# Mixer A/B of a hybrid trunk: turns of channel blocks by DMA in place of engine copies, and a new order of states, outputs, gate and projection

## The chip, the cores and the metric

The kernel runs on one core of a Trainium2 chip. The metric is the device time of one execution in microseconds (us); the median of three runs of the kernel before is 2035.25 us (2034.42 to 2035.31).

## What is computed

Two decoder layers over 512 tokens of width 1024. The change touches one place alone, the mixer of the first layer, where a short gated convolution (A) and a diagonal state space (B) share an input and an output projection:

```python
proj = h @ ab_w_in[j]
hc, gb, gc, u = jnp.split(proj, [CONV_CH, 2 * CONV_CH, 3 * CONV_CH], axis=-1)
ya = short_conv_mixer(hc, gb, gc, conv_w[j])        # gb * conv3(gc * hc)
yb = s5_mixer(u, ...)                               # 32 groups of 16 channels, 64 states each
mix = jnp.concatenate([ya, yb], axis=-1) @ ab_w_out[j]

# s5_mixer, after the scan over the tokens:
z = jax.nn.gelu(y)
out = z * jax.nn.sigmoid(z @ w_glu + b_glu)
```

The two feed-forward blocks, the layer norms, the second layer's attention and the gated embeddings are the same in both kernels.

## The kernel before, in words

Activations lie with channels on the partitions, in tiles of 128 channels by 512 tokens. Every product is made of three matmuls on high and low halves (`xh,whi`, `xl,whi`, `xh,wlo`), so a product of one 128-channel output tile over K = 1024 is 24 matmuls of 512 columns; the text calls it a whole. Weights come as a stream of 128 x 1024 pieces (`Stream`): SyncE issues a load into one of 3 raw buffers, ScalarE casts the high half (`whi`, L77), VectorE subtracts for the low half (`wlo`, L78), and the halves lie in a ring of 7. A load must wait for the `wlo` of the piece three earlier, since that frees its raw buffer. After each use of a piece, `free` issues one more load and one more split, so loads, casts and subtractions stand in their engines' queues at that place of the program.

The mixer's pieces are numbered here w0 to w25: w0 to w3 make the four tiles of u (`group`), then for ct = 0 to 3 come `hc`, `gc` and `gb` (hc0 is w4, gc0 w5, gb0 w6, ... gb3 w15), then the gate (`w_glu`), the first half of the output projection and its tail. `hc` is copied out of PSUM by ScalarE (L832); `gc` is multiplied and convolved by VectorE (L839 to L843); `gb` is multiplied in (L848), and the result split into `Y`. The four PSUM banks "U" hold the results of wholes in turn.

The state space needs time on another axis: groups of 32 channels by every fourth token. A turn moves sixteen blocks of 32 partitions x 128 between a tile and its turned form, `ut` from `us` and `z` from `y`. Before, each turn is 16 copies (L764), 8 on ScalarE and 8 on VectorE. For a tile f of u:

- `states(f)`: 8 products from `ut[f]` and `pack[f]` into two banks "D" (L777; the trace counts 16 records), then on VectorE 6 multiplications and additions, 8 scans, and 6 more, into `hz[f]` (L783 to L805).
- `output(f)`: 12 products (24 records) into a bank "L" (L815, L817), Gelu on ScalarE (`y`, L819), the turn to `z[f]`, the split into `Y`, and the load of `pack[f+2]` (1792 KB, L744), which takes the place of `pack[f]`; there are two pack buffers.

The gate is 48 matmuls over all of `z` and a sigmoid, a product and a split for each tile (L868, L869). The first half of the output projection has eight outputs (`down`), added to `u` (L422). The `tail` then makes the second half together with the layer norm; it opens with L143. `self.at(ns, f)` puts f into the order when `ns` of matmul time have been written behind it.

The order of the work is written by hand, in `plan`. A turn of the tiles of u is called `along`.

Of the kernel before, what the change touches and what calls it, by code (L numbers as in the profile page):

```python
# [10 lines left out]
F = mybir.dt.float32  # L11
R = mybir.dt.float32r
I32 = mybir.dt.int32
AF = mybir.ActivationFunctionType
OP = mybir.AluOpType

P = 128
T = 512
# [181 lines left out]
class Program:  # L200
# [23 lines left out]
    def pair(self):  # L224

        return tuple(self.pairs.tile([P, KD, T], R, name=f"x{s}", tag=f"x{s}") for s in "hl")
# [502 lines left out]
    def mixer_ab(self, ln):  # L729
        nc, ws, a = self.nc, self.ws, self.a  # L730
        v = nc.vector
        es = ExitStack()
        pool = es.enter_context(self.tc.tile_pool(name="ab", bufs=1))
        small = pool.tile([P, 16], F, name="small")
        nc.gpsimd.dma_start(small, a["abs"])
        bglu, cw = small[:, 0:4], small[:, 4:16].rearrange("p (c j) -> p c j", j=3)
        ut = [pool.tile([P, 4, P], F, name=f"ut{f}") for f in range(4)]
        us, z = {}, {}
        Y = self.pair()
        packs = {}  # L740

        def load(f):
            packs[f] = pool.tile([P, 3584], F, name="pack", tag="pack", bufs=2)
            nc.sync.dma_start(packs[f], self.s5d[f])  # L744

        load(0)
        load(1)

        def have_u(m, b):
            for i in range(2):  # L750
                us[m + i] = pool.tile([P, 4, P], F, name="us", tag="uz", bufs=4)
                nc.scalar.copy(us[m + i], b[i].rearrange("p (k t) -> p t k", t=4))
            if m == 0:
                along(0)

        def along(f):

            x = us.pop(f)
            turn_steps(lambda q, t: (ut[f][32 * t:32 * t + 32, q, :], x[32 * q:32 * q + 32, t, :]))

        def turn_steps(pair):
            for q in range(4):
                for t in range(4):
                    (nc.scalar.copy if t % 2 else nc.vector.tensor_copy)(*pair(q, t))  # L764

        self.group(have_u)
        self.pending = False
        hz = {}

        def states(f):  # L770
            pk = packs[f]
            SB = pk[:, 1024:2048].rearrange("p (r q s) -> p r q s", r=2, q=4)
            b = [self.bank("D") for _ in range(2)]
            uu = ut[f]
            for r in range(2):
                for q in range(4):
                    nc.tensor.matmul(b[r][:, q * P:(q + 1) * P], lhsT=SB[:, r, q, :], rhs=uu[:, q, :],  # L777
                                     start=True, stop=True)
            c, s = pk[:, 0:512], pk[:, 512:1024]
            t1 = self.work.tile([P, 2, T], F, name="m1", tag="t4")  # L780
            t2 = self.work.tile([P, 2, T], F, name="m2", tag="t4")
            zz = pool.tile([P, 2, T], F, name="zz")
            v.tensor_mul(t1[:, 0], b[0], c)  # L783
            v.tensor_mul(t1[:, 1], b[1], s)
            v.tensor_add(zz[:, 0], t1[:, 0], t1[:, 1])
            v.tensor_mul(t2[:, 0], b[1], c)
            v.tensor_mul(t2[:, 1], b[0], s)
            v.tensor_sub(zz[:, 1], t2[:, 0], t2[:, 1])
            for r in range(2):
                for q in range(4):  # L790
                    x = zz[:, r, q * P:(q + 1) * P]
                    v.tensor_tensor_scan(x, self.s5r[:, 4 * f + q:4 * f + q + 1].to_broadcast([P, P]), x, 0.0,  # L792
                                         op0=OP.mult, op1=OP.add)
            h = pool.tile([P, 2, 4, P + 2], F, name="hz", tag="hz", bufs=2)
            hz[f] = h
            nc.gpsimd.memset(h[:, :, :, 0:1], 0.0)
            t1 = self.work.tile([P, 2, T], F, name="m1", tag="t4")
            t2 = self.work.tile([P, 2, T], F, name="m2", tag="t4")
            v.tensor_mul(t1[:, 0], zz[:, 0], c)
            v.tensor_mul(t1[:, 1], zz[:, 1], s)  # L800
            v.tensor_mul(t2[:, 0], zz[:, 0], s)
            v.tensor_mul(t2[:, 1], zz[:, 1], c)
            t1, t2 = (t.rearrange("p r (q k) -> p r q k", q=4) for t in (t1, t2))
            v.tensor_sub(h[:, 0, :, 1:P + 1], t1[:, 0], t1[:, 1])
            v.tensor_add(h[:, 1, :, 1:P + 1], t2[:, 0], t2[:, 1])  # L805

        def output(f):
            pk = packs.pop(f)
            CB = pk[:, 2048:3072].rearrange("p (r q s) -> p r q s", r=2, q=4)
            KB = pk[:, 3072:3584].rearrange("p (q s) -> p q s", q=4)  # L810
            b = self.bank("L")
            h = hz.pop(f)
            for q in range(4):
                o = b[:, q * P:(q + 1) * P]
                nc.tensor.matmul(o, lhsT=KB[:, q], rhs=ut[f][:, q], start=True, stop=False)  # L815
                for r in range(2):
                    nc.tensor.matmul(o, lhsT=CB[:, r, q], rhs=h[:, r, q, 0:P], start=False, stop=r == 1)  # L817
            y = self.work.tile([P, 4, P], F, name="y", tag="t4")
            nc.scalar.activation(y.rearrange("p q k -> p (q k)"), b, AF.Gelu_apprx_tanh)  # L819
            z[f] = pool.tile([P, T], F, name="z", tag="uz", bufs=4)  # L820
            zf = z[f].rearrange("p (k t) -> p t k", t=4)
            turn_steps(lambda q, t: (zf[32 * q:32 * q + 32, t, :], y[32 * t:32 * t + 32, q, :]))
            self.split_pair(Y, 4 + f, z[f])
            if f + 2 < 4:
                load(f + 2)

        conv = {}

        def hc(ct):
            b = self.whole()  # L830
            conv[ct] = pool.tile([P, T], F, name="hc")
            nc.scalar.copy(conv[ct], b)  # L832

        def gc(ct):
            b = self.whole()
            uu = pool.tile([P, T + 2], F, name="uu")
            vv = pool.tile([P, T], F, name="vv")
            nc.gpsimd.memset(uu[:, 0:2], 0.0)
            v.tensor_mul(uu[:, 2:], conv[ct], b)  # L839
            conv[ct] = vv  # L840
            v.tensor_scalar(vv, uu[:, 0:T], cw[:, ct, 0:1], None, op0=OP.mult)
            for j in (1, 2):
                v.scalar_tensor_tensor(vv, uu[:, j:j + T], cw[:, ct, j:j + 1], vv, op0=OP.mult, op1=OP.add)  # L843

        def gb(ct):
            b = self.whole()
            vv = conv.pop(ct)
            v.tensor_mul(vv, vv, b)  # L848
            self.split_pair(Y, ct, vv)

        plan = [(hc, 0), (along, 1), (states, 0), (along, 2), (gc, 0), (along, 3), (states, 1), (gb, 0), (hc, 1),
                (output, 0), (gc, 1), (output, 1), (gb, 1), (states, 2), (hc, 2), (gc, 2), (states, 3), (gb, 2),
                (hc, 3), (output, 2), (gc, 3), (output, 3), (gb, 3)]
        for f, i in plan:
            f(i)

        self.lows()
        banks = []
        for i in range(2):
            w = ws.take()  # L860
            for s in range(2):
                b = self.bank("U")
                self.mm(b, w, Y, range(4 * s, 4 * s + 4), range(4, 8), slice(0, T))
                banks.append(b)
            ws.free()
        for f in range(4):
            t = self.work.tile([P, 2, T], F, name="gl", tag="t4")
            nc.scalar.activation(t[:, 0], banks[f], AF.Sigmoid, bias=bglu[:, f:f + 1])  # L868
            v.tensor_mul(t[:, 1], t[:, 0], z[f])  # L869
            self.split_pair(Y, 4 + f, t[:, 1])  # L870
        self.lows()
        for j in range(KD):
            if j % 2 == 0:
                w = ws.take()
            self.down(w, (j % 2) * 4, Y, range(4), j, True)
            if j % 2:
                ws.free()
        self.tail(Y, 4, ln)
        es.close()

# [365 lines left out]
def cut_rows(w, k0, k1):  # L1246

    k, m = w.shape
    n = 8 // (k1 - k0)
    w = w.reshape(k // P, P, m // P, P)[k0:k1].transpose(1, 2, 0, 3)  # L1250
    return [w[:, j:j + n].reshape(P, 1024) for j in range(0, m // P, n)]
# [21 lines left out]
def pieces_ab(w_in, w_glu, w_out):  # L1273
    t = tiles_of(w_in)
    out = t[12:16]
    for c in range(4):
        out += [t[c], t[8 + c], t[4 + c]]
    return out + cut_rows(w_glu, 0, 4) + cut_rows(w_out, 0, 4) + cut_tail(w_out, 4)


def pieces_ple(wp, wg):
# [117 lines left out]
```

## Time and profile before

| | |
|---|---|
| median of the three runs | 2035.25 us |
| the profiled execution, its own time | 2035.52 us |
| its span, first to last instruction | 2033.8 us |
| TensorE busy (matmuls) | 98% of the span |
| VectorE, ScalarE, GpSimd busy | 52%, 34%, 5% |
| granted TensorE clock, mean | 0.993 |

Times in the rows count from the start of the span. The mixer's work that the change touches runs from 408.6 us (the first tiles of u are done) to 553.2 us (the tail opens). The granted clock is 1.00 in nearly all of the span; it has two levels, 1.2 and 2.4 GHz, and a mean between 0.5 and 1 in a stretch is a mix of the two.

### The profile page before, as it was taken

The numbers are of one execution on the slowest core, as the hardware profiler recorded it, in microseconds if no ns is written. First come the engines' busy times: TensorE is split into PE (matmuls) and PEld (weight loads), VectorE is DVE, ScalarE is ACT, GpSimd is POOL, SyncE is SP. The second block draws the span as 40 slices with busy tenths as digits, with TensorE's granted clock in tenths as the row PEclk, the third lists the DMA queues.
The fourth block names the chain that finished last, engine by engine and source line by source line (L and its number), as shares of the span: only waits on it lengthen the run. The fifth ranks groups of instructions, "written<-read, shape, count | busy, mean of one in ns | idle before, by whom it ended". The sixth has DMA issues, their size and how long they took to land.

```text
span 2033.8 us, 23989 instructions
## 1 busy us (share of the span) xinstructions
PE 1986.0 (98%) x9550; PEld 1645.0 (81%) x9550; DVE 1066.5 (52%) x2027; ACT 684.1 (34%) x1026; POOL 94.3 (5%) x89
## 2 busy tenths in 40 slices
PE   9999999999899999999999999998999999999999
PEld 7888888877688888887888888887777888888877
DVE  6457554678554333336645554356986543333363
ACT  5222332444343222224432222234444432222242
POOL 0001110000000000000000000002431000000000
PEclk9999999999899999999999999999999999999999
DMA  6234343323314232321332322312211142323312
GB/s 218 95 104 145 115 134 114 126 89 129 99 37 137 91 103 89 104 99 42 119 114 85 105 101 87 104 69 83 74 52 45 49 135 93 104 84 103 103 42 73
DMA packets 54736, 197.99 MB, mean 97 GB/s; under 512 B 6529, under 2 KB 6817, under 8 KB 54113
## 3 DMA queue, kind: packets, MB, share of 16 engines
q1 hardware_dynamic: 51840, 187.74, 27.5%
q0 software_dynamic: 2640, 8.67, 1.2%
q8 instruction: 75, 1.23, 0.3%
q14 instruction: 37, 0.30, 0.0%
q10 hardware_dynamic: 144, 0.05, 0.0%
HBM read 187.00 MB, written 9.44 MB: 97 GB/s over the span
## 4 chain that ended last, share of the span: by engine, by line
PE 64%; DVE 8%; ACT 4%; issue 2%; POOL 0%; DMA 0%; DVEq 0%; ACTq 0%; POOLq 0%
PE U L260 44%; PE D L260 15%; PE D L443 1%; PE U L443 1%; DVE wlo L78 1%; ACT u L188 1%; ACT whi L77 1%; PE D L1110 1%; ACT lnt L173 1%; PE U L1079 1%; DVE xl L197 0%; DVE lnst L150 0%; PE L L180 0%; ACT xh L190 0%; DVE zz L792 0%
## 5 line engine op out<-in xcount | busy, mean ns | idle before, releaser
L260 PE MATMUL U<-xh,whi 128*128 128x512 f32 (+1 forms) x2000 | 751.4, 376 | 6.3 <-ACT xh L319 5.3
L260 PE MATMUL U<-xl,whi 128*128 128x512 f32 (+1 forms) x2000 | 745.2, 373 | 5.4 <-DVE xl L326 4.1
L260 PE MATMUL U<-xh,wlo 128*128 128x512 f32 (+1 forms) x2000 | 744.3, 372 | 0.0
L78 DVE TENSOR_TENSOR wlo<-wraw,whi 128x1024 fp32r<-128x1024 f32 (+1 forms) x321 | 393.6, 1232 | 303.3 <-ACT whi L77 301.8
L77 ACT CAST whi<-wraw 128x1024 fp32r<-128x1024 f32 (+1 forms) x337 | 350.6, 1045 | 559.7 <-PE D L260 309.3
L260 PEld LDWEIGHTS U<-xh,whi 128*128 128x128 f32 x2000 | 378.0, 189 | 76.5 <-ACT xh L319 6.4
L260 PEld LDWEIGHTS U<-xl,whi 128*128 128x128 f32 x2000 | 377.9, 189 | 73.9 <-DVE xl L326 6.4
L260 PEld LDWEIGHTS U<-xh,wlo 128*128 128x128 f32 x2000 | 377.8, 189 | 65.1
L260 PE MATMUL D<-xh,whi 128*128 128x512 f32 x608 | 237.6, 391 | 1.4 <-DVE u L422 1.0
L260 PE MATMUL D<-xh,wlo 128*128 128x512 f32 x608 | 236.6, 389 | 0.0
L260 PE MATMUL D<-xl,whi 128*128 128x512 f32 x608 | 236.6, 389 | 0.0
L373 DVE SCALAR_TENSOR_TENSOR gt<-gt,U 128x512 f32<-128x512 f32 x88 | 60.4, 687 | 265.8 <-PE U L260 208.8
L319 ACT CAST xh<-gt 128x512 fp32r<-128x512 f32 x88 | 54.6, 620 | 387.9 <-DVE gt L373 387.9
L260 PEld LDWEIGHTS D<-xh,whi 128*128 128x128 f32 x608 | 114.1, 188 | 27.7 <-DVE u L424 3.0
L260 PEld LDWEIGHTS D<-xh,wlo 128*128 128x128 f32 x608 | 114.2, 188 | 23.9
L260 PEld LDWEIGHTS D<-xl,whi 128*128 128x128 f32 x608 | 114.2, 188 | 23.3
L424 DVE TENSOR_TENSOR u<-u,D 128x512 f32<-128x512 f32 x64 | 43.9, 687 | 112.2 <-PE D L260 112.2
L422 DVE SCALAR_TENSOR_TENSOR u<-u,D 128x512 f32<-128x512 f32 x40 | 27.4, 687 | 108.1 <-PE D L260 108.1
L326 DVE TENSOR_TENSOR xl<-gt,xh 128x512 fp32r<-128x512 f32 x88 | 60.3, 685 | 8.2 <-ACT xh L319 8.2
L372 ACT ACTIVATE gt<-U 128x512 f32<-128x512 f32 x88 | 51.9, 589 | 18.4 <-PE U L260 18.3
L186 DVE TENSOR_SCALAR u<-L,lnw 128x128 f32<-128x128 f32 x96 | 32.8, 404 | 32.6 <-PE L L180 32.6
L173 ACT ACTIVATE lnt<-D,lnm,lny 128x512 f32<-128x512 f32 x24 | 17.4, 773 | 72.3 <-DVE lnm L170 72.3
(318 smaller groups left out, 1593.3 us busy)
## 6 DMA issues: line engine op xcount, KB each, us to landing
wraw<-wts SPq DMA_DIRECT2D x333, 512.0 KB, 3.5
pack<-s5d SPq DMA_DIRECT2D x4, 1792.0 KB, 9.4
s5d<-big POOLq DMA_DIRECT2D x20, 256.0 KB, 5.0
u<-x SPq DMA_DIRECT2D x8, 256.0 KB, 5.3
s5d<-big POOLq DMA_DIRECT2D x4, 512.0 KB, 3.3
out<-u SPq DMA_DIRECT2D x7, 256.0 KB, 2.0
wraw<-wts SPq DMA_DIRECT2D x4, 256.0 KB, 5.5
pt<-p POOLq DMA_DIRECT2D x2, 512.0 KB, 4.5
```

What stands on the lines that cost most here:

```text
L77: self.nc.scalar.copy(hi, t)
L78: self.lo_engine.tensor_sub(lo, t, hi.bitcast(F))
L173: p.nc.scalar.activation(self.z[:, c], self.banks[c], AF.Identity, bias=m, scale=y)
L186: p.nc.vector.tensor_scalar(out, x, gam, bet, op0=OP.mult, op1=OP.add)
L260: self.nc.tensor.matmul(out, lhsT=p[:, s], rhs=q[:, xk, cols], start=first and i == 0 and j == 0, stop=last and i == n - 1 and j == 2)
L319: self.nc.scalar.copy(hi[:, j, :], src)
L326: self.nc.vector.tensor_sub(out, src, hi)
L372: nc.scalar.activation(t[:, 0], pa, AF.Silu)
L373: nc.vector.scalar_tensor_tensor(t[:, 1], t[:, 0], 0.5, pb, op0=OP.mult, op1=OP.mult)
L422: self.nc.vector.scalar_tensor_tensor(u, u, ALPHA, d, op0=OP.mult, op1=OP.add)
L424: self.nc.vector.tensor_add(u, u, d)
L443: self.nc.tensor.matmul(b, lhsT=x, rhs=y, start=False, stop=k == TAIL - 1 and j == 2)
```

## The change

Three things. The turns are 16 DMAs of 32 x 128 each, from SBUF to SBUF, in place of 16 copies: on SyncE's queue, for `ut[0]` alternately on SyncE's and ScalarE's. A tile of `z` now has its tokens in turned order, and the gate's product puts them back (a view with a stride of four). The order is a new one: `states(0)` is put into hc0 (1500 ns after it begins), `states(1)`, (2), (3) behind gb0, gb1, gb2, `output(0)`, (1), (2) behind gc1, gc2, gc3, and `output(3)` behind the second output of the projection. Turns of `z` are put 1500 ns behind their output, the splits of `z` 9000 ns. Six of the projection's eight outputs are made before the gate's products, two behind them; the pieces of `w_out` and `w_glu` change places to suit.

```diff
+        def turn(out, src, engines):
+            for j in range(4):
+                for i in range(4):
+                    engines[(4 * j + i) % len(engines)].dma_start(out[32 * i:32 * i + 32, j, :], src[32 * j:32 * j + 32, i, :])
...
             for i in range(2):
-                us[m + i] = pool.tile([P, 4, P], F, name="us", tag="uz", bufs=4)
-                nc.scalar.copy(us[m + i], b[i].rearrange("p (k t) -> p t k", t=4))
-            if m == 0:
-                along(0)
-        def along(f):
-            x = us.pop(f)
-            turn_steps(lambda q, t: (ut[f][32 * t:32 * t + 32, q, :], x[32 * q:32 * q + 32, t, :]))
-        def turn_steps(pair):
-            for q in range(4):
-                for t in range(4):
-                    (nc.scalar.copy if t % 2 else nc.vector.tensor_copy)(*pair(q, t))
+                us = pool.tile([P, 4, P], F, name="us", tag="uz", bufs=4)
+                nc.scalar.copy(us, b[i].rearrange("p (k t) -> p t k", t=4))
+                turn(ut[m + i], us, (nc.sync,) if m + i else (nc.sync, nc.scalar))
...
-            z[f] = pool.tile([P, T], F, name="z", tag="uz", bufs=4)
-            zf = z[f].rearrange("p (k t) -> p t k", t=4)
-            turn_steps(lambda q, t: (zf[32 * q:32 * q + 32, t, :], y[32 * t:32 * t + 32, q, :]))
-            self.split_pair(Y, 4 + f, z[f])
+            z[f] = pool.tile([P, 4, P], F, name="z", tag="uz", bufs=4)
+            self.at(1500, turn, z[f], y, (nc.sync,))
+            self.at(9000, lambda: self.split_pair(Y, 4 + f, z[f].rearrange("p t k -> p (t k)")))
...
-        plan = [(hc, 0), (along, 1), (states, 0), (along, 2), (gc, 0), (along, 3), (states, 1), (gb, 0), (hc, 1),
-                (output, 0), (gc, 1), (output, 1), (gb, 1), (states, 2), (hc, 2), (gc, 2), (states, 3), (gb, 2),
-                (hc, 3), (output, 2), (gc, 3), (output, 3), (gb, 3)]
-        for f, i in plan:
-            f(i)
+        self.at(1500, states, 0)
+        for ct in range(4):
+            for i, f in enumerate((hc, gc, gb)):
+                f(ct)
+                n = 3 * ct + i
+                if n in (2, 5, 8):
+                    states(n // 3 + 1)
+                if n in (4, 7, 10):
+                    output(n // 3 - 1)
...
             self.down(w, (j % 2) * 4, Y, range(4), j, True)
             if j % 2:
                 ws.free()
+            if j == 1:
+                output(3)
+            if j == 5:
+                self.flush()
+                gates()
```

On SyncE's queue, from the first two packs on (`wraw` a weight piece, `pack<-s5d_1396` and `_1397` the third and fourth pack), the kernel before has:

```order
L744 DMA pack<-s5d_1395 128x3584
L70 DMA wraw<-wts 128x1024 x10
L744 DMA pack<-s5d_1396 128x3584
L70 DMA wraw<-wts 128x1024
L744 DMA pack<-s5d_1397 128x3584
L70 DMA wraw<-wts 128x1024 x252
```

The changed kernel has, in the same place:

```order
L744 DMA pack<-s5d_1395 128x3584
L70 DMA wraw<-wts 128x1024 x2
L753 DMA ut_3055<-us 32x128 x8
L753 DMA ut_3056<-us 32x128 x16
L70 DMA wraw<-wts 128x1024 x2
L753 DMA ut_3057<-us 32x128 x16
L753 DMA ut_3058<-us 32x128 x16
L70 DMA wraw<-wts 128x1024 x7
L744 DMA pack<-s5d_1396 128x3584
L753 DMA z<-y 32x128 x16
L70 DMA wraw<-wts 128x1024 x3
L744 DMA pack<-s5d_1397 128x3584
```

The ten pieces ahead of the third pack are w6 to w15 before and the eleven of the change w6 to w16. Of the pieces, w8 and w9 now stand behind the turns of the first two tiles, w10 to w16 behind all four; the fourth pack moved from behind w16 to behind w19. Each DMA of the change also waits, on its queue, for the landing of the one issued eight before it, by the semaphores that the build gives them.

On VectorE, from the second chain of states on (`hz` is what `output(1)` waits for), the kernel before has:

```order
L804 TENSOR_TENSOR hz<-m_3529 128x4x128
L805 TENSOR_TENSOR hz<-m_3530 128x4x128
L78 TENSOR_TENSOR wlo<-wraw,whi 128x1024
L848 TENSOR_TENSOR vv<-vv,U 128x512
L78 TENSOR_TENSOR wlo<-wraw,whi 128x1024
L326 TENSOR_TENSOR xl<-vv,xh 128x512
L764 COPY z<-y 32x128 x8
```

The changed kernel has between the first chain's end and the second chain's start, and behind its end:

```order
L801 TENSOR_TENSOR hz<-m_3432 128x4x128
L78 TENSOR_TENSOR wlo<-wraw,whi 128x1024 x2
L834 TENSOR_TENSOR uu<-hc,U 128x512
L836 TENSOR_SCALAR vv<-uu,small 128x512
L838 SCALAR_TENSOR_TENSOR vv<-uu,small,vv 128x512 x2
L78 TENSOR_TENSOR wlo<-wraw,whi 128x1024
L843 TENSOR_TENSOR vv<-vv,U 128x512
L779 TENSOR_TENSOR m_3543<-D,pack 128x512
...
L801 TENSOR_TENSOR hz<-m_3563 128x4x128
L78 TENSOR_TENSOR wlo<-wraw,whi 128x1024
```

The first `wlo` behind the second chain is that of w12 before and that of w13 in the change; the three `wlo` between the two chains are those of w10, w11 and w12, together with the convolution of gc0 and the product of gb0. Ahead of the first chain stand the `wlo` of w8 and w9 in the change, of w8 to w10 before.

## Rows read from the trace of the kernel before

**Rows 1.** The page's busy times by engine, over the whole span.

```profile
PE 1986.0 (98%) x9550; PEld 1645.0 (81%) x9550; DVE 1066.5 (52%) x2027; ACT 684.1 (34%) x1026; POOL 94.3 (5%) x89
```

**Rows 2.** Waits of PE, 340 to 640: who waited for whom, total us, times, longest.

```profile
PE U L260 <- ACT xh L319: 4.9, 1, 4.9
PE U L260 <- DVE xl L326: 3.7, 2, 2.0
...
PE D L777 <- DVE m L786: 2.6, 1, 2.6
PE D L777 <- issue: 2.0, 1, 2.0
PE L L817 <- DVE hz L804: 1.4, 1, 1.4
PE D L777 <- DMA pack<-s5d: 1.3, 1, 1.3
```

**Rows 3.** Timeline of PE, 408 to 560: start, us, line, records [idle before].

```profile
411.68 0.40 PE L260 MATMUL U<-xh,whi 128*128 128x512 f32 x1
...
417.14 1.95 PE L777 MATMUL D<-ut,pack 128*128 128x128 f32 x16
418.84 0.48 PE L260 MATMUL U<-xh,whi 128*128 128x512 f32 x1
...
441.55 0.38 PE L815 MATMUL L<-ut,pack 128*128 128x128 f32 x2
...
444.14 0.48 PE L260 MATMUL U<-xh,whi 128*128 128x512 f32 x1
...
476.26 3.65 PE L777 MATMUL D<-ut,pack 128*128 128x128 f32 x16 [2.04 <-issue]
479.66 0.48 PE L260 MATMUL U<-xh,whi 128*128 128x512 f32 x1
...
553.15 0.60 PE L143 MATMUL D<-ident,u 128*128 128x128 f32 x4
```

**Rows 4.** Busy us by engine in a stretch, then granted clock, DMA share, GB/s.

```profile
475.00:480.00 5.00, 3.74 (x18) 3.73 (x19) 4.96 (x13) 2.60 (x4) 0.00 (x0) 0.66 0.04 16
```

**Rows 5.** Line L764, the turn's copies: ns min/median/max, first and last start.

```profile
L764 DVE COPY ut<-us x32: 207/218/222, 409.3 to 441.6; 32x128 f32<-32x128 f32 x32
L764 ACT COPY ut<-us x32: 293/296/299, 409.7 to 430.0; 32x128 f32<-32x128 f32 x32
L764 ACT COPY z<-y x32: 409/414/429, 457.7 to 512.1; 32x128 f32<-32x128 f32 x32
L764 DVE COPY z<-y x32: 264/272/278, 457.7 to 515.1; 32x128 f32<-32x128 f32 x32
```

**Rows 6.** Timeline of SyncE's DMA queue, 445 to 480.

```profile
453.11 0.33 SPq L70 DMA_DIRECT2D wraw<-wts  x1
453.49 0.42 SPq L744 DMA_DIRECT2D pack<-s5d  x1
```

**Rows 7.** From issue to landing, lines L70 (weights), L744 (packs), L1230 (output).

```profile
DMA to landing us min/median/max: 3.3/3.5/8.0
...
DMA to landing us min/median/max: 7.7/9.4/12.3
...
DMA to landing us min/median/max: 1.7/2.0/2.1
```

**Rows 8.** Timeline of DVE, 405 to 460, around the first two chains of states.

```profile
424.25 0.69 DVE L783 TENSOR_TENSOR m<-D,pack 128x512 f32<-128x512 f32 x1
...
434.25 1.83 DVE L764 COPY ut<-us 32x128 f32<-32x128 f32 x8
...
437.25 0.68 DVE L839 TENSOR_TENSOR uu<-hc,U 128x512 f32<-128x512 f32 x1
...
440.01 1.83 DVE L764 COPY ut<-us 32x128 f32<-32x128 f32 x8
...
451.87 1.22 DVE L78 TENSOR_TENSOR wlo<-wraw,whi 128x1024 fp32r<-128x1024 f32 x1
```

More of the change, by code (lines that the diff above doesn't have):

```diff
@@ L737, in mixer_ab @@
         ut = [pool.tile([P, 4, P], F, name=f"ut{f}") for f in range(4)]
-        us, z = {}, {}
+        z = {}
         Y = self.pair()
@@ L849, in gb, with gates @@
             self.split_pair(Y, ct, vv)
-        plan = [(hc, 0), (along, 1), (states, 0), (along, 2), (gc, 0), (along, 3), (states, 1), (gb, 0), (hc, 1),
-                (output, 0), (gc, 1), (output, 1), (gb, 1), (states, 2), (hc, 2), (gc, 2), (states, 3), (gb, 2),
-                (hc, 3), (output, 2), (gc, 3), (output, 3), (gb, 3)]
-        for f, i in plan:
-            f(i)
[L857 to L870, printed above, removed]
+        def gates():
+            self.lows()
+            banks = []
+            for i in range(2):
+                w = ws.take()
+                for s in range(2):
+                    b = self.bank("U")
+                    self.mm(b, w, Y, range(4 * s, 4 * s + 4), range(4, 8), slice(0, T))
+                    banks.append(b)
+                ws.free()
+            for f in range(4):
+                t = self.work.tile([P, 2, T], F, name="gl", tag="t4")
+                nc.scalar.activation(t[:, 0], banks[f], AF.Sigmoid, bias=bglu[:, f:f + 1])
+                v.tensor_mul(t[:, 1].rearrange("p (k t) -> p t k", t=4), t[:, 0].rearrange("p (t k) -> p t k", t=4), z[f])
+                self.split_pair(Y, 4 + f, t[:, 1])
+        self.at(1500, states, 0)
[7 more added lines that the diff above has]
+                    output(n // 3 - 1)
         self.lows()
@@ L877, in mixer_ab @@
                 ws.free()
+            if j == 1:
[3 more added lines that the diff above has]
+                gates()
+        self.lows()
         self.tail(Y, 4, ln)
@@ L1277, in pieces_ab @@
         out += [t[c], t[8 + c], t[4 + c]]
-    return out + cut_rows(w_glu, 0, 4) + cut_rows(w_out, 0, 4) + cut_tail(w_out, 4)
+    first = cut_rows(w_out, 0, 4)
+    return out + first[:3] + cut_rows(w_glu, 0, 4) + first[3:] + cut_tail(w_out, 4)
 def pieces_ple(wp, wg):
```

## The prediction

> **What bounds the kernel now.** I read the page's busy times first: TensorE is busy for 98% of the span, so only a stretch where it idles can give anything [rows 1]. The waits of TensorE around the mixer name that stretch: six kinds, 4.9 + 3.7 + 2.6 + 2.0 + 1.4 + 1.3 = 15.9 us [rows 2]. The first two end on the split of z or vv into Y (L319, L326), behind copies of a turn; the third and fourth are states that wait for a turn or for VectorE.
>
> The timeline then prices the stage. A whole takes 417.14 - 411.68 = 5.46 us, 0.2275 a matmul; the products of one states 418.84 - 417.14 = 1.70; of one output 444.14 - 441.55 = 2.59 [rows 3]. From hc0 to the tail there are 12 wholes, 4 states, 4 outputs, 48 gate matmuls and eight outputs of 12 matmuls: 65.5 + 6.8 + 10.4 + 10.9 + 21.8 = 115.4 us. It takes 553.15 - 411.68 = 141.5 [rows 3]. So 26.1 us are lost: 15.9 in those waits, the rest mostly in slow matmuls behind them. One such place: after 2.04 idle the states took 479.66 - 476.26 = 3.40 in place of 1.70, in a stretch whose mean granted clock is 0.66 of 2.4 GHz [rows 3, 4]. With every wait gone the kernel would gain 26; the question is which waits the new order makes.
>
> **The copies removed.** ScalarE loses 32 x 0.296 + 32 x 0.414 = 22.7 us, VectorE 32 x 0.218 + 32 x 0.272 = 15.7 [rows 5]. Neither is on the path by itself; what they free is the head of Y's splits, and those waits (8.6 us) go. Moving output(3) behind two projections and the gate behind six does the same for z3. I charge nothing there: z3 has four projections, 10.9 us, between its Gelu and the gate.
>
> **The turns added.** A turn is 16 DMAs of 16 KB. The trace has no such DMA. Bounds for a turn: by landing, eight may be in flight and the output's stores land in 2.0 us at the median [rows 7], so two rounds, 4.0 us. By issue, two neighbours on SyncE start 453.49 - 453.11 = 0.38 apart [rows 6], so 16 x 0.38 = 6.1. Those move 128 rows where a turn's move 32, so the issue should be cheaper than that row; I take 5.0.
>
> The landing row is the one that a page speaks to. The Trainium skill ("DMA: Bandwidth & Descriptors", section on the anatomy of one DMA) gives a DMA a fixed part of about 2.0 us and says in its measured table that transfers under 64 KB are dominated by descriptors, which speaks against 128 of them; by its formula an estimate is 2.04 us for 16 KB and 4.1 for a turn, and the gain below would be 8.3 in place of 7.4. The shortest landing here, 1.7, agrees in size, though for stores to memory and not SBUF to SBUF [rows 7].
>
> What a turn delays is the queue behind it. us0 is there at 409.3, the first start of a copy of it [rows 5]. ut0 lands two rounds later, about 413.8 to 414.4; states(0) is placed 9 matmuls into hc0, at 413.7, so 0.5 us wait. ScalarE issues eight of these DMAs in order, so us1 is copied only at about 412.8. ut1 then takes SyncE to 417.8, and only there come w8 and w9 (before, w8 was loaded long ahead). They land 3.5 later [rows 7], the second about 1.3 behind the first; cast and subtraction take 1.1 and 1.2. w9's wlo ends at about 424.9.
>
> **VectorE's chain sets the packs.** In the new order the first chain of states stands behind that wlo: it starts at 424.9, against 424.25 before [rows 8], though its products are done by 416. The chain takes 434.25 - 424.25 = 10.0 [rows 8]. Behind it: wlo of w10 and w11 (1.15 each), convolution 440.01 - 437.25 = 2.76 [rows 8], wlo of w12 and the product of gb0 1.75, the second chain 10.0, wlo of w13 1.15. That is 424.9 + 10.0 + 2.3 + 2.76 + 1.75 + 10.0 + 1.15 = 452.9. Only then may w16 be issued, and the third pack stands behind w16 on SyncE: issue at 453.3. The kernel before shows the same queueing: its third pack went out at 453.49, right behind a weight that waited for the wlo of 451.87 to 453.09, though output(0) had left the buffer at 444.14 [rows 3, 6, 8]. The shortest pack landing is 7.7 [rows 7], and I take that, since no other pack is in flight: 461.0.
>
> What changed is who waits. Before, output(1) stood between; states(2) waited 1.3 [rows 2]. Now states(2) comes one whole after output(0). TensorE: 414.2 + 1.7 (states(0)) + 3.4 (rest of hc0) + 10.9 + 1.7 (states(1)) + 10.9 + 2.6 (output(0)) + 5.5 = 450.9. It waits 461.0 - 450.9 = 10.1 us.
>
> **The rest of the stage.** After that wait the clock is low: states(2) 3.4 as at 476.26 and 0.5 more in hc2, so 464.4 and 475.8 after hc2 and gc2, 478.4 after output(1). z0's DMAs follow the third pack and land about 463 to 465, ahead of the m tile that takes y's buffer (VectorE, about 472). w16's wlo ends about 476.3, ahead of 478.4, so w19 and the fourth pack go out at 478.5 and land at 486.2; gb2 ends at 483.9: a wait of 2.3, and 2.2 again for the clock. From 486.2: 3.4 + 0.5 + 10.9 + 2.6 + 5.5 (gb3) + 5.4 + 2.6 (output(3)) + 10.9 + 10.9 (gate) + 5.4 = 544.3. Each change of tile costs about 0.1 more at its first matmul, some 12 of them: 545.5. The chain sigmoid, product, split for the gate runs beside the last two projections (5.4 us) and its last split is wanted 2 us into the tail; I charge 0.3. The tail opens at 545.8 in place of 553.15: **a gain of 7.4 us**. The rest of the program is bound by TensorE and keeps its time.
>
> The profiled execution's own time is 2035.52 (span 2033.8 and 1.7 around it); less 7.4 it is 2028.1. Against the median, 0.3 lower, I forecast **2027.8**.
>
> **Rivals.** First, **slow turns**, which end slower than before. Up to a turn of 5.5 us only ut1 counts, 1 us for 1 us. Beyond it w10 is late, behind ut2 and ut3: it is issued at 413.6 + 3 turns, its wlo ends 5.7 later, VectorE stands still between the chains, and hc0's copy, which is queued on ScalarE behind w10's cast, holds a U bank. The third pack lands 25.0 behind that wlo. At 6.1 a turn this is 462.6 and the gain 5.8; at 8.1, 0.5 us a DMA, it is nothing; at 10 it is 474.3, 13.3 later, which is 5.9 slower than before: 2041. For it: weights on a shared queue land in up to 8.0 us [rows 7], and eight in flight at 5 us each is 10 a turn. Against it: 0.38 an issue and 2.0 a landing.
>
> Second, **late packs**: if both land in the 12.3 of the longest pack landing [rows 7] and not in 7.7, TensorE waits 4.6 longer twice: 2027.8 + 9.2 = 2037.0. For it: turns share the queue and the memory ports with the packs. Against: that longest one had another pack ahead of it.
>
> Third, **the whole gain**: the packs are there in time. Then about 6 us of the 26.1 remain, for ut0 and the tile changes: 2015. It would need the third pack out by 443, and VectorE's queue above denies it by 10 us.
>
> **How the numbers follow.** Forecast (2021 to 2032; a turn of 4.0 to 6.5 us, packs of 7.7 to 9.4): 0.58. Slow turns (2036 to 2046): 0.16. Late packs (2032 to 2038): 0.16. The whole gain (2013 to 2021): 0.10. About 0.2%, 4.1 us, is what a measurement of this kernel can tell from no change. Faster by more, below 2031.2: 0.10 and nearly all of 0.58, with little of late packs, 0.66. Slower by more, above 2039.3: most of slow turns and little else, 0.16. Within: 0.18. The range 2018 to 2038 leaves out about half of the third rival and most of the first.
>
> **What would show it.** In the changed kernel's trace: a wait of about 10 us of TensorE at the third states, ended by the pack, and one of about 2 at the fourth; the third pack issued right behind a weight load and a wlo, near 453; the first chain of states starting near 425, behind w9's wlo; no long wait on Y's splits at the gate; a turn of 4 to 6 us on SyncE; the tail opening near 546. Wrong would be: a pack landing before 451, a first chain starting with its products at 416, or a turn above 8 us.

## The result: 0.77% slower

| | before | after |
|---|---|---|
| median, us | 2035.28 (2034.42 to 2035.93, 4 runs) | 2050.86 (2049.72 to 2052.08, 4 runs) |
| ratio after / before, 95% interval | | 1.0077 [1.0059, 1.0094] |
| span of the profiled execution, us | 2033.8 | 2047.9 |
| the tail of the projection opens, us | 553.15 [rows 3] | 567.11 |

The forecast was 2027.8 with a range to 2038.0, so the sign is wrong. The span grew by 14.1 us and the opening of the tail moved by 13.96: the loss lies inside the stage that the prediction looked at, and the rest of the program kept its time.

The computing engines have no more work than before; ScalarE lost 22 us of copies (684.1 busy before, [rows 1]). The page of the changed kernel, busy times:

```profile
PE 1986.2 (97%) x9550; PEld 1644.6 (80%) x9550; DVE 1052.7 (51%) x1963; ACT 661.6 (32%) x962; POOL 94.4 (5%) x89
```

What grew are waits. The waits of TensorE in the changed kernel, 340 to 660 (who waited for whom: total us, times, longest), to be held against [rows 2]:

```profile
PE D L773 <- DMA z<-y: 10.6, 1, 10.6
PE U L260 <- ACT hc L827: 8.5, 1, 8.5
PE D L773 <- issue: 3.9, 1, 3.9
...
PE D L773 <- DMA pack<-s5d: 2.3, 1, 2.3
PE U L260 <- DVE xl L326: 2.3, 1, 2.3
PE D L143 <- DVE u L422: 1.5, 1, 1.5
PE D L773 <- DMA ut<-us: 1.2, 2, 0.6
PE U L260 <- ACT xh L319: 0.4, 1, 0.4
```

The 4.9 on `xh` and 3.7 on `xl` of before are nearly gone, as the change would have it. In their place stand 10.6 at the third states, 8.5 at a U bank and 3.9 at the second states: 30.7 in these eight rows, 15.9 in the six of [rows 2].

The first row is a lesson in reading: L773 computes states from `ut` and `pack` and never touches z. The wait is put down to the last transfer that landed; it is the pack that the states needed. The pack landed 7.8 us after its issue at 472.00, at 479.8, and the states started at 480.03. SyncE's own queue shows what held that pack up (start, us from the first to the end of the last issue, DMAs):

```profile
409.89 16.04 SPq L753 DMA_DIRECT2D ut<-us  x24
426.03 1.00 SPq L70 DMA_DIRECT2D wraw<-wts  x2
427.12 21.31 SPq L753 DMA_DIRECT2D ut<-us  x32
448.53 23.38 SPq L70 DMA_DIRECT2D wraw<-wts  x7
472.00 0.38 SPq L744 DMA_DIRECT2D pack<-s5d  x1
...
521.96 10.02 SPq L753 DMA_DIRECT2D z<-y  x16
```

A row is to be divided by its count: 21.31 / 32 = 0.67 us from one DMA to the next, 10.02 / 16 = 0.63. A turn costs SyncE 10.0 to 10.7 us, in place of 5.0. (The first two turns of z took 13.8 and 13.6: their eighth DMA waits for the landing of the pack issued eight before it, and SyncE's waits for the pack are 3.1 and 2.3 us.) All 56 of the u turns go ahead of w10 to w16, and the third pack stands behind w16: it is issued at 472.00, where the forecast had 453.3. The line of the turns itself, ns of one issue (min, median, max), then us from issue to landing:

```profile
L753 SPq DMA_DIRECT2D ut<-us x56: 507/588/1528, 409.9 to 447.8; - x56
...
DMA to landing us min/median/max: 1.7/1.8/7.6
```

They land in 1.8 us at the median, so none of the u turns had to wait for the landing of the one eight before it (eight issues take 5 us). What takes the time is issuing them one after the other. Nor did the turns slow the weights on their way: from 405 to 580 us a weight landed 3.4, 3.8 and 5.1 us after its issue (least, median, most), against 3.4, 3.6 and 5.8 before.

The way from w10 to TensorE, in the timelines of ScalarE, VectorE and TensorE of the changed kernel (start, us, line, operation, records [idle before and what ended it]):

```profile
452.22 1.04 ACT L77 CAST whi<-wraw 128x1024 fp32r<-128x1024 f32 x1 [19.89 <-DMA wraw<-wts]
453.17 0.58 ACT L827 COPY hc<-U 128x512 f32<-128x512 f32 x1
```

```profile
453.29 1.22 DVE L78 TENSOR_TENSOR wlo<-wraw,whi 128x1024 fp32r<-128x1024 f32 x1 [9.73 <-ACT whi L77]
...
470.34 1.21 DVE L78 TENSOR_TENSOR wlo<-wraw,whi 128x1024 fp32r<-128x1024 f32 x1
```

```profile
453.80 0.79 PE L260 MATMUL U<-xh,whi 128*128 128x512 f32 x1 [8.46 <-ACT hc L827]
...
480.03 3.75 PE L773 MATMUL D<-ut,pack 128*128 128x128 f32 x16 [10.64 <-DMA z<-y]
...
505.69 2.02 PE L773 MATMUL D<-ut,pack 128*128 128x128 f32 x16 [2.34 <-DMA pack<-s5d]
...
567.11 0.66 PE L143 MATMUL D<-ident,u 128*128 128x128 f32 x4 [1.53 <-DVE u L422]
```

w10's cast ends ScalarE's idle 19.9 us; the copy of hc0 is queued right behind it, and TensorE has waited 8.5 for the bank that this copy reads. The first chain of states had started at 433.50, behind w9's `wlo` as forecast, but 8.6 later than the 424.9 of the forecast. VectorE then stood still for 9.7 ahead of w10's `wlo`, and runs from there the chain that the prediction laid out, to the `wlo` of 470.34 that lets w16 and the pack go. TensorE's third states start at 480.03 (forecast 461.0), the tail 21.3 later than forecast.

### The profile page after: what moved, and what is told of

Its sections match the earlier page's. It is cut to its first block, busy times and chain, and to the rows that moved or that the text cites. A ratio compares the mean times of both kernels' runs of the same rounds, so it can differ in the third digit from the quotient of the medians.

```text
span 2047.9 us, 24052 instructions
## 1 busy us (share of the span) xinstructions
PE 1986.2 (97%) x9550; PEld 1644.6 (80%) x9550; DVE 1052.7 (51%) x1963; ACT 661.6 (32%) x962; POOL 94.4 (5%) x89
## 4 chain that ended last, share of the span: by engine, by line
PE 66%; DVE 6%; ACT 3%; issue 1%; DMA 1%; POOL 0%; SPq 0%; DVEq 0%; ACTq 0%; POOLq 0%
PE U L260 45%; PE D L260 15%; PE D L443 1%; PE U L443 1%; ACT u L188 1%; PE D L1118 1%; ACT lnt L173 1%; PE U L1087 1%; DVE wlo L78 1%; ACT whi L77 1%; DVE xl L197 0%; DVE lnst L150 0%; PE L L180 0%; ACT xh L190 0%; DMA pack<-s5d 0%
## 5 line engine op out<-in xcount | busy, mean ns | idle before, releaser
L260 PE MATMUL U<-xh,whi 128*128 128x512 f32 (+1 forms) x2000 | 751.4, 376 | 10.1 <-ACT hc L827 8.5
L422 DVE SCALAR_TENSOR_TENSOR u<-u,D 128x512 f32<-128x512 f32 x40 | 27.4, 686 | 107.8 <-PE D L260 107.8
L78 POOL TENSOR_TENSOR wlo<-wraw,whi 128x1024 fp32r<-128x1024 f32 x16 | 38.3, 2405 | 67.7 <-PE U L260 44.6
```

The source lines that it names most:

```text
L78: self.lo_engine.tensor_sub(lo, t, hi.bitcast(F))
L260: self.nc.tensor.matmul(out, lhsT=p[:, s], rhs=q[:, xk, cols], start=first and i == 0 and j == 0, stop=last and i == n - 1 and j == 2)
L422: self.nc.vector.scalar_tensor_tensor(u, u, ALPHA, d, op0=OP.mult, op1=OP.add)
```

## Experiments

The theory after the result, **the queue theory**: a turn by DMA occupies its in-order issuing queue for 10 us, and the weights and packs behind it come late; nothing else of the change costs. Its rivals: **the order theory** (the new order itself loses, whatever makes the turns), **the row theory** (the forecast's: few rows should issue cheaply, so something else slowed these), and **the weights theory** (only the place of two weight loads behind the turns matters). A variant that ran once has no interval; its time stands beside the median of the kernel before on the same chip (2035.86 to 2036.21). Executions of one kernel lie up to 4.4 us apart here (2028.89 to 2033.31), so a smaller difference of a single execution decides nothing by itself.

### The new order with copies

```diff
-                    engines[(4 * j + i) % len(engines)].dma_start(out[32 * i:32 * i + 32, j, :], src[32 * j:32 * j + 32, i, :])
+                    (nc.scalar.copy if i % 2 else nc.vector.tensor_copy)(out[32 * i:32 * i + 32, j, :], src[32 * j:32 * j + 32, i, :])
```

> The changed kernel with its order, but each turn again 16 copies (8 ScalarE, 8 VectorE) in the place where the change issues 16 DMAs. Queue theory (the turns' issues, 0.67 us each in the changed kernel, hold up weights and packs behind them on SyncE): the weights w8 to w11 land in time, the 8.5 us wait for hc0's copy is gone, a wait of about 10 us for the third pack stays, time 2026 to 2034. Order theory (the new order itself costs, by states one whole behind the output that frees their pack): time stays at 2045 or more.

2029.79 us (2027.14 to 2031.36, 8 runs), ratio to before 0.9969 [0.9959, 0.9980]. So the order gains 6 us, and the DMAs lose 21 on top. Its SyncE queue, TensorE's waits and TensorE's timeline:

```profile
454.64 0.42 SPq L744 DMA_DIRECT2D pack<-s5d  x1
```

```profile
PE D L773 <- DMA pack<-s5d: 13.2, 2, 11.3
...
PE U L260 <- DVE xl L326: 0.3, 1, 0.3
```

```profile
462.14 3.75 PE L773 MATMUL D<-ut,pack 128*128 128x128 f32 x16 [11.31 <-DMA pack<-s5d]
...
545.60 0.66 PE L143 MATMUL D<-ident,u 128*128 128x128 f32 x4 [1.49 <-DVE u L422]
```

This is nearly the forecast's schedule (pack out at 453.3, third states at 461.0, tail at 545.8), reached with the copies that the change took away.

### The order of before with DMA turns

The kernel before, with its plan and the gate ahead of the projection, but with every turn as 16 DMAs on SyncE, the splits of z 9000 ns behind, and the gate's product on the turned view.

```diff
-                    (nc.scalar.copy if t % 2 else nc.vector.tensor_copy)(*pair(q, t))
+                    nc.sync.dma_start(*pair(q, t))
...
```

> The kernel before with its order, but each turn 16 DMAs on SyncE (splits of z 9000 ns behind, the gate's product with the turned view). Queue theory: weights stand behind turns here too, so waits of TensorE grow and the time is 2043 to 2060. Order theory: without the new order the time is near 2035.

2056.39 in one execution: 20.5 above before. The DMA turns cost about 20 us in either order, so the order theory falls. The longest waits are now at the states, 11.5 for the turns themselves and 9.0 that the profile puts down to no one:

```profile
PE D L777 <- DMA ut<-us: 11.5, 5, 5.4
PE D L777 <- issue: 9.0, 1, 9.0
```

### One half of the turns at a time

u alone by DMA, z by copies; and the other way round.

```diff
-            self.at(1500, turn, z[f], y, (nc.sync,))
+            self.at(1500, copies, z[f], y)
```

> The changed kernel with DMA turns for u alone; z is turned by copies in the place of its DMAs. Queue theory: w8 to w16 stand behind 56 DMAs as in the changed kernel, so the wait for hc0's copy of about 8.5 us and the late third pack stay: 2042 to 2050. If z's turns are the larger part, 2034 or less.

```diff
-                turn(ut[m + i], us, (nc.sync,) if m + i else (nc.sync, nc.scalar))
+                copies(ut[m + i], us)
```

> The changed kernel with DMA turns for z alone; u is turned by copies in place. Queue theory: weights up to w16 and the third pack go out as in e1_copies, and z's turns delay only w17 and later, which have slack: 2029 to 2035. If z's turns are the larger part of the 20 us, 2040 or more.

u alone: 2046.49 in one execution, 16.7 above the kernel with copies, with the third pack issued at 471.54 and the same waits of 8.2 (hc's bank), 4.0 and 10.7 (the third states). z alone: 2039.19, 9.4 above, 4 more than expected. Its third states start 1.0 later than with copies (463.15, 462.14), its second output 2.2 (478.84, 476.66), which holds the fourth pack's buffer; the fourth states start 2.8 later and take 3.65 in place of 2.02; the last split of z costs 2.3 at the gate. About 2 us of its 8.7 at the tail I could not place. Both halves cost; together (21.1) they cost less than the sum (26.1), and both delay the same packs; that this is the reason was not tested.

### What an issue costs

Behind the end of the kernel before stand 33 DMAs on SyncE: the store of a tile, and 4 each of eight kinds. They add some 20 us to the time (2055.88); only their durations count.

```diff
+    for j in range(4):
+        nc.sync.dma_start(a128[:, j, :], src[:, j, :])
...
+        nc.sync.dma_start(a16[0:16, j, :], src[32:48, j, :])
...
+        nc.sync.dma_start(w32[32 * j:32 * j + 32], src[32 * j:32 * j + 32])
...
+        nc.sync.dma_start(d32[0:32, j, :], dram[32:64, j, :])
...
+        nc.sync.dma_start(out[0:32, j, :], src[32:64, j, :])
```

> The kernel before with 33 DMAs behind its end on SyncE's queue, 4 of each shape: SBUF to SBUF of 128, 64, 32 and 16 rows of 512 B, 32 rows of 2 KB, memory to SBUF of 32 and 128 rows of 512 B, SBUF to memory of 32 rows of 512 B. It measures the issue alone. Row theory: the cost goes with the rows, and 32 rows cost less than 128 (as the forecast took): 0.1 to 0.3 us. Few-rows theory: 32 rows cost 0.5 to 0.6 wherever they lie, 128 rows 0.33. SBUF theory: SBUF to SBUF costs 0.5 to 0.6 at every number of rows, memory to SBUF 0.33.

Lines of the probe, ns of one issue (min, median, max). In order: SBUF to SBUF of 128 and of 16 rows with 512 B each, of 32 rows with 2 KB each; memory to SBUF of 32 rows; SBUF to memory of 32 rows. The 32 rows of 512 B that a turn moves took 590 at the median, 64 rows 593, memory to SBUF of 128 rows 430.

```profile
L1374 SPq DMA_DIRECT2D pra<-psrc x4: 562/592/599, 2032.9 to 2034.8; - x4
...
L1380 SPq DMA_DIRECT2D pra<-psrc x4: 507/584/589, 2040.9 to 2042.7; - x4
...
L1382 SPq DMA_DIRECT2D prw<-psrc x4: 587/588/588, 2043.3 to 2045.2; - x4
...
L1384 SPq DMA_DIRECT2D prd<-pdram x4: 419/420/578, 2045.8 to 2047.4; - x4
...
L1389 SPq DMA_DIRECT2D pout<-psrc x4: 419/420/432, 2049.7 to 2051.1; - x4
```

Neither rows (16 to 128) nor bytes (8 to 64 KB) change the price. What does is whether one end is in memory: 0.42, or both in SBUF: 0.59. The SBUF theory holds, with 0.42 for memory to SBUF where it had 0.33. The row theory falls, and with it the step of the forecast that took 5.0 because "the issue should be cheaper than that row".

### The turn through memory

The changed kernel with its order untouched: a turn is one store of the tile to memory and four loads of 32 rows, 5 DMAs for 16.

```diff
+        bounce = [self.dram.tile([P, 4, P], F, name=f"bounce{i}") for i in range(8)]
...
+            d = bounce.pop()
+            engines[0].dma_start(d, src)
             for j in range(4):
-                for i in range(4):
-                    engines[(4 * j + i) % len(engines)].dma_start(out[32 * i:32 * i + 32, j, :], src[32 * j:32 * j + 32, i, :])
+                engines[0].dma_start(out[32 * j:32 * j + 32], d.rearrange("(i p) j k -> p i j k", i=4)[:, :, j, :])
```

> The changed kernel, order untouched, but a turn goes through memory: one store of the tile (128 rows) and four loads of 32 rows x 4 x 512 B, all on SyncE, five issues in place of sixteen. With the issue costs of e6_issue_cost (0.33 and 0.42, the first load waiting 2 us for the store) a turn holds SyncE about 4.4 us, near the 5.0 of the forecast, in place of the 10.6 measured in the changed kernel. Queue theory: the time is the forecast's, 2024 to 2032, with a wait of 10 to 12 us for the third pack and none over 2 for hc0's copy. If DMA turns cost by their bytes or their landing, and not by the issues ahead of the weights, it stays above 2042.

2029.72 us (2028.89 to 2033.31, 10 runs), ratio 0.9975 [0.9965, 0.9984]. SyncE's queue, then TensorE's waits and timeline:

```profile
413.80 0.38 SPq L754 DMA_DIRECT2D bounce<-us  x1
415.89 1.73 SPq L756 DMA_DIRECT2D ut<-bounce  x4
...
418.66 0.38 SPq L754 DMA_DIRECT2D bounce<-us  x1
423.87 1.75 SPq L756 DMA_DIRECT2D ut<-bounce  x4
...
453.85 0.38 SPq L744 DMA_DIRECT2D pack<-s5d  x1
```

```profile
PE D L776 <- DMA bounce<-y: 9.4, 1, 9.4
...
PE D L776 <- DMA pack<-s5d: 2.2, 1, 2.2
```

```profile
462.03 3.75 PE L776 MATMUL D<-ut,pack 128*128 128x128 f32 x16 [9.38 <-DMA bounce<-y]
...
546.16 0.66 PE L143 MATMUL D<-ident,u 128*128 128x128 f32 x4 [1.54 <-DVE u L422]
```

From 413.80 to the end of the loads at 417.62 the second turn keeps SyncE 3.8 us, 1.7 of them a wait for its own store. The third takes 7.0 (418.66 to 425.62), since its store, issued right behind two weights, lands only after 5.2; the four of u take 4.7 on average, close to the 5.0 of the forecast. (The first two of z take 10.0 and 9.3: their stores, issued right behind a pack, land after 8.2 and 7.5.) With that one price changed, the pack goes out at 453.85, the waits are 9.4 (again put down to the last transfer) and 2.2, and the tail opens at 546.16: forecast 453.3, 10.1, 2.3 and 545.8. The theory that the bytes or the landing cost (above 2042) falls.

### The turns on another queue, and the weights first

All turns on GpSimd's queue:

```diff
-                    engines[(4 * j + i) % len(engines)].dma_start(out[32 * i:32 * i + 32, j, :], src[32 * j:32 * j + 32, i, :])
+                    nc.gpsimd.dma_start(out[32 * i:32 * i + 32, j, :], src[32 * j:32 * j + 32, i, :])
```

> The changed kernel with every turn's DMAs issued on GpSimd's queue, which is idle in the mixer, in place of SyncE's and ScalarE's. Queue theory: weights and packs go out in time; if GpSimd's issue costs no more than about 0.7 us, the time is 2026 to 2036, with the third pack's wait of about 10 us left. Order theory: still 2045 or more. If the transfers themselves are slow (a third theory, contention of small DMAs with the loads), weights land later than 5 us also here.

2039.04 in one execution, 3 above the range: 12 better than on SyncE, 9 worse than copies. The weights ahead of the pack are in time and hc0's bank is not waited for. But GpSimd issues at about 0.5 us each, and TensorE waits 4.7 for the first turns. GpSimd's queue was not idle either: it holds small memsets, and one of 0.12 us, which fills the edge of `uu`, stood behind all 64 DMAs of the u turns until 443.02. VectorE waited 7.9 for it between the two chains, so w16 and the third pack went out only at 458.50 (454.64 with copies). It is the same mechanism on another queue. TensorE's waits, then VectorE's timeline:

```profile
PE D L773 <- DMA pack<-s5d: 11.7, 2, 8.4
PE D L773 <- DMA ut<-us: 4.7, 2, 3.1
```

```profile
443.17 0.49 DVE L836 TENSOR_SCALAR vv<-uu,small 128x512 f32<-128x512 f32 x1 [7.92 <-POOL hz L792]
```

On SyncE, but each two weights are issued ahead of the turns of their pair:

```diff
-                    if h and k0:
+                    if h and k0 and early:
+                        ws.free(2)
+                        done(m, p[m:m + 2])
+                    elif h and k0:
...
-        self.group(have_u)
+        self.group(have_u, True)
```

> The changed kernel with the loads and splits that follow a pair of u tiles put ahead of that pair's copies and turns, so that w8 to w11 go out ahead of the turns on SyncE. Queue theory: the first chain of states starts 5 us earlier or more, the 8.5 us wait for hc0's copy is gone, and the time is 2036 to 2044; the third pack is still late. Order theory: 2050, no change.

2048.06 in one execution, 4 above the range. The waits of 8.5 and 3.9 are gone, so these came from the two weights behind the turns. Yet one wait took nearly all of it over, since w12 to w16 and the pack still stand behind the last 32 DMAs:

```profile
448.32 18.19 SPq L70 DMA_DIRECT2D wraw<-wts  x5
466.60 0.38 SPq L747 DMA_DIRECT2D pack<-s5d  x1
```

```profile
PE D L776 <- DMA z<-y: 23.6, 2, 21.6
```

The weights theory falls: the pack sets the time of the third states, and a wait removed ahead of it only makes the wait for it longer.

### The pack off SyncE's queue

If the third pack's place behind w16 is what costs the kernel with copies its 11.3 us, another queue should free it. GpSimd's has only memsets of about 0.1 us there.

```diff
-            nc.sync.dma_start(packs[f], self.s5d[f])
+            (nc.sync if f < 2 else nc.gpsimd).dma_start(packs[f], self.s5d[f])
```

> The new order with turns by copies (as e1_copies), and the third and fourth pack loaded on GpSimd's queue in place of SyncE's, where they stand behind w16 and w19. Queue theory: the third pack goes out when output(0) ends, near 445 in place of 454.6, and lands near 453; the 11.3 us wait falls under 4, time 2018 to 2025. If the wait is set by output(0) or by the transfer itself, it stays above 8 and the time near 2029.

**2021.74** us (2021.44 to 2023.60, 4 runs), ratio 0.9932 [0.9915, 0.9948], the fastest of all. GpSimd's timeline and TensorE's waits:

```profile
445.67 0.54 POOL L744 DMA_DIRECT2D pack<-s5d  x1 [4.05 <-PE L L813]
```

```profile
PE D L773 <- DMA pack<-s5d: 2.6, 1, 2.6
PE D L773 <- DVE vv L838: 2.5, 1, 2.5
```

The pack goes out when TensorE's first output releases its buffer, 9 us earlier than behind w16, and the tail opens at 538.88.

The next step cut each pack in two, so that the states' part can be loaded as soon as the states two earlier have done with theirs:

```diff
-            (nc.sync if f < 2 else nc.gpsimd).dma_start(packs[f], self.s5d[f])
+            packs[f] = pool.tile([P, 2048], F, name="packs", tag="packs", bufs=2)
+            (nc.sync if f < 2 else nc.gpsimd).dma_start(packs[f], self.s5d[f][:, 0:2048])
...
+            if f + 2 < 4:
+                load(f + 2)
...
```

> As e5_pack_pool, with a pack cut into the part that states read (1024 KB) and the part that output reads (768 KB): the first is loaded as soon as the states two earlier have run through VectorE, on GpSimd's queue. The 2.6 us wait for the third pack goes; VectorE's chain (the 2.5 us wait at the fourth states) stays. 2017 to 2021; if VectorE alone sets these places, no gain over e5_pack_pool, 2022.

2023.78 us (2023.29 to 2024.10, 4 runs): a miss, 2 slower at the median than the version before it, though the two ranges touch; its tail opens 1.6 later. The waits of 2.6 and 2.5 are gone, and one of 8.1 opened at the projection, behind VectorE. VectorE works without a gap from 484 until the product, ending at 501.8, that the last convolved tile of Y is split from; its waits, then its timeline:

```profile
PE D L260 <- ACT xh L319: 8.1, 1, 8.1
```

```profile
501.13 0.68 DVE L850 TENSOR_TENSOR vv<-vv,U 128x512 f32<-128x512 f32 x1
```

Last, the fastest version with the gate put ahead of all eight projection outputs, as it stood before:

```diff
+        output(3)
+        self.flush()
+        gates()
         self.lows()
         for j in range(KD):
...
-            if j == 1:
-                output(3)
-            if j == 5:
-                self.flush()
-                gates()
...
-    return out + first[:3] + cut_rows(w_glu, 0, 4) + first[3:] + cut_tail(w_out, 4)
+    return out + cut_rows(w_glu, 0, 4) + first + cut_tail(w_out, 4)
```

> As e5_pack_pool, but output(3) and the gate stand ahead of all eight outputs of the projection, as in the kernel before. The gate then waits for z3: Gelu, copies, split, about 6 us with the low clock behind it. 2027 to 2031. If the placing of the projection is worth nothing, 2022.

2026.77 in one execution, 5.0 slower, a little under the range; the tail opens 5.2 later, and TensorE waits 4.0 for a split at the gate. So in this version the place of the projection around the gate is worth some 5 us; what it is worth in the changed kernel itself was not tried.

## Why the prediction was wrong, step by step

- **The failing step: "I take 5.0" for a turn.** Of the two bounds, 4.0 by landing and 6.1 by issue, the true one was issue, and above the upper end: 16 x 0.63 to 0.67 = 10.0 to 10.7. The row behind 0.38 was a load from memory [rows 6]; a turn has both ends in SBUF, and the probe gives 0.59 for that against 0.42. The argument from rows (32 against 128) had no row of the trace behind it, and the probe shows no such effect. The range's upper end for a turn, 6.5, fell with it, and what followed was the delay that the prediction had worked out for longer turns: w10 went out at 448.53, and the third pack at 472.00 in place of 453.3.
- **The slow-turns rival was the mechanism, at too small a size.** It had 2041 at 10 us a turn. Two terms were short: us1 was copied at 415.30 in place of 412.8, since ScalarE's eight issues cost it 5.4 us, and a turn is up to 10.7. So w10 went out at 448.53, by the rival's formula at 443.6. From there it holds: w10's `wlo` ends at 454.5, and 25.0 later is 479.5; the third states started at 480.03. The break-even was put at 0.5 us a DMA, and its chance of 0.16 was low for a price that no row bounded from above.
- **The landing estimate was about right and decided nothing.** The turns landed in 1.8 us at the median. By the formula of the Trainium skill ("DMA: Bandwidth & Descriptors", section on the anatomy of one DMA), which that section fits to DMAs issued from GpSimd and the prediction used for SyncE, the estimate was 2.04 us for 16 KB; the table that the prediction names is of loads from memory, also issued from GpSimd. What counted is the issue, 0.59 us in the probe and 0.63 to 0.67 from one to the next, against 1.8 for one landing: for 16 in a row it is all of the turn. The Trainium skill (the same page, section "Issuing engines are not separate DMA queues") calls the sequencer's time to start a DMA usually small beside the DMA itself; for these DMAs the measurement says otherwise.
- **VectorE's chain to the pack held.** With turns of 4.7 us for u (through memory) or by copies, the first chain started at 425.4 and 426.3 (forecast 424.9), and pack, waits and tail came within 1.4 us of the forecast. That is an experiment on this one term, not only an argument. That the tail came within 0.4 is in part luck, as the last two points show.
- **The copies removed were worth nothing.** The new order with copies (2029.79) and with cheap DMA turns (2029.72) take the same time. I had charged nothing for the 22.7 and 15.7 us themselves, but credited their absence with the 8.6 us of waits on Y's splits; the order removes these by itself (0.3 is left with copies).
- **z3, charged nothing, and the gate, charged 0.3.** In the changed kernel the last split of z costs 2.3, since its turn takes 10.6 of SyncE; with copies 0.3. The gate's product on the turned view takes 1.07 in place of 0.69 us, four times, which the prediction did not look at. The tail then waits 1.5 for VectorE's `u` (L422), which is queued behind the last of them. Where the gate stands ahead of the projection, TensorE waits 1.0 for `u` in the kernel before and 2.4 in the two versions with the turned view, so some 1.4 us of the product seems to show; it was not tried alone.
- **The fourth pack's wait, the clock after the long wait, and the rest of the program** came as forecast: 2.3 us of wait; 483.44 - 480.03 = 3.41 us for the states after the long wait (3.4 forecast), at a granted clock of 0.50 of 2.4 GHz, the lower of the two levels, after 10.6 us in which TensorE stood still; nothing outside the stage. The stretch, in the columns of [rows 4]:

```profile
480.00:484.00 4.00, 3.97 (x17) 3.91 (x18) 0.87 (x2) 0.00 (x0) 0.00 (x0) 0.50 0.10 26
```

- **The clock after the fourth wait did not.** The prediction charged 2.2 us for it. The fourth states took 1.78 us from their start to the next whole (505.69 to 507.47) at a granted clock of 1.00, and the same with copies and through memory. These 2.2 us too many hid the 1.2 too few for the gate and third states that came some 1 us late: the tail at 545.60 and 546.16 owes its closeness to 545.8 to that.

What stays open: some 2 us of the kernel with z alone, and how far the fastest version could go with VectorE's queue reordered, which was not tried; so is the exact share of the gate's slower product.

## What to carry to other kernels

Price many small DMAs by what the issuing queue needs for them, with a row of the same kind at both ends (memory or SBUF), and list what is queued behind them on that queue: here 56 issues of 0.67 us, not their bytes, made the weights and a pack late. Where a row for the price is missing, the range has to reach to where the sign turns. Before freeing engines of work, look whether anyone waits for them; moving two late loads to a nearly idle queue (8 us) was worth more than 38 us of copies. Before moving many issues to another engine's queue, list the small work of that engine behind them too: one memset of 0.12 us held VectorE for 7.9.

## What the runs showed of the hardware

- The issue of a DMA cost SyncE 0.59 us with both ends in SBUF, for 16 to 128 rows and 512 B or 2 KB a row, 0.42 with one end in memory for parts of a tile, 0.33 to 0.42 for a whole tile, weight or pack [rows 6]. GpSimd took 0.5 for the same SBUF transfers, and 0.54 for a pack.
- Small DMAs issued right behind a pack land late: the first seven of z's turn landed 4.9 to 7.6 us after their issue, against 1.8 at the median of all turns.
- Eight DMAs on ScalarE's queue kept ScalarE itself for 5.4 us, and the copy of us1 queued behind them waited that long.
- VectorE's product of 128 x 512 took 1.07 us when its output steps by 16 bytes, 0.69 otherwise. The Trainium skill ("SBUF — State Buffer", the note on cachelines in the section on the DMA port swizzle) says that each access that crosses to a new 16-byte line pays a penalty. These rows agree, the first of the changed kernel, the second of before:

```profile
L860 DVE TENSOR_TENSOR gl<-gl,z x4: 1062/1071/1080, 557.6 to 564.9; 128x512 f32<-128x512 f32 x4
```

```profile
L869 DVE TENSOR_TENSOR gl<-gl,z x4: 691/692/693, 527.7 to 534.0; 128x512 f32<-128x512 f32 x4
```
